# Issuing the last SiLU and product of an up chunk behind the copy of the next chunk's first product

## The chip, the core and the metric

The program runs on one core of a Trainium2 chip. The metric is the device time of one execution in microseconds, lower being better. A core has TensorE (PE, the matrix multiplier, with PEld for its weight loads), VectorE (DVE), ScalarE (ACT), GpSimd (POOL) and SyncE (SP), each with its own queue worked off in order; an instruction that waits holds up everything behind it on its engine. Results of TensorE land in PSUM, which VectorE and ScalarE read; everything else is in SBUF.

## The reference

The program is an encoder trunk of two layers over 768 tokens (512 of one request, 256 of another), with 1024 features. Each layer is `x += 1/2 FFN(norm(x)); x += mixer(norm(x)); x += 1/2 FFN(norm(x))`; the mixers are a gated linear recurrence and a windowed attention. The four feed-forwards are what matters here:

```python
def swiglu_ffn(x, w1, w2):
    gate, up = jnp.split(x @ w1, 2, axis=-1)      # w1: 1024 x 5632
    return (jax.nn.silu(gate) * up) @ w2          # w2: 2816 x 1024
```

Everything is float32. The kernel splits each operand into a high and a low part and multiplies three times (high by high, high by low, low by high).

## The kernel before

**Tiling.** The 2816 hidden features are 22 chunks of 128. A feed-forward (`ffn`, L510) goes through five groups of four chunks and then two more chunks. A group computes the hidden values of its four chunks ("up"), and then multiplies them into the output ("down", `down_quad`, L465). The first two chunks of a feed-forward are computed plainly; every later one by `up_pair` (L431), which makes seven products of half the depth (p1, p7, p2, p5, p4, p6, p3, in this order) in place of eight. So a full group has four calls of `up_pair`, here called its chunks 1 to 4; the first group has only chunks 3 and 4.

**One chunk.** A product is twelve matmuls of 128x384 (L422). Products accumulate in four PSUM banks a, b, c, d, and some banks are read in the middle: ScalarE copies bank a after p1 (L439, "the copy") because p2 goes on accumulating in the same bank, so p2's first matmul waits for the copy; likewise c after p7 (L442). After p6, VectorE combines the banks (L452 to L454), giving the first half's hidden value t. After p3 come L457 and L459 on VectorE, the SiLU of the second half on ScalarE (L460) and its product on VectorE (L461), giving w.

**After a chunk.** Each half is split into high and low (ScalarE L267, then VectorE L268). After two chunks `gather` calls `mix`, four VectorE subtractions (L351, L352, L354, L355) over the four halves with three more splits, giving the combined operands t1 to t4 that "down" takes.

**Down.** Seven products of 18 matmuls of 128x512 (L486), in the order p1, p2, p5, p4, p7, p6, p3 of the source. VectorE adds each partial result into x (L508). p2 goes on accumulating in p1's banks, and p4 in p5's, so p2's first matmul waits for the first L508 on p1, and p4's for that on p5.

**Weights.** Each weight block is loaded by SP into one of four raw buffers `wr` (L155), then staged into one of eight tiles `w`: ScalarE makes the high part (L203), VectorE the low part (L204; for p5 of an up chunk it is GpSimd). Some products need sums of blocks: two VectorE additions in the raw buffer (L217: one for p6, then one for p3), and additions made by DMAs that POOL issues (L145). A raw buffer is loaded anew when the last reader of its block is done: for an up chunk that is the L204 of p3. The four raw buffers of a "down" are filled while chunks 2 to 4 run. The third weight of "down" (p5's) is a sum that POOL's DMA makes from the third and the fourth raw buffer.

**What sets the order.** The instructions are written in program order and a scheduler places them on each engine's queue by when it takes them to be ready; `issue_after` adds an order between two instructions without a wait. `up_pair` is a generator: it yields t and later w, and the caller splits and gathers between.

Of the kernel before, what the change touches and what calls it, by code (L numbers as in the profile page):

```python
# [12 lines left out]
AF = mybir.ActivationFunctionType  # L13
# [35 lines left out]
class Trunk:  # L49
    def __init__(self, ctx, tc, consts):  # L50
        self.tc, self.nc = tc, tc.nc
        pool = lambda name, **kw: ctx.enter_context(tc.tile_pool(name=name, bufs=1, **kw))
        self.cp = pool("consts")
        self.xp = pool("xp")
        self.wp = pool("wp")
        self.tp = pool("tp")
        self.sp = pool("stats")
        self.ap = pool("arena")
        self.pp = pool("psum", space=bass.MemoryType.PSUM)
        self.dp = pool("dram", space=bass.MemoryType.DRAM)  # L60
        self.uid = 0
        self.deferred = []
        self.queue, self.loaded, self.staged, self.held = [], [], {}, 0
        self.setup(consts)

# [362 lines left out]
                    skip_group_check=True,  # L428
                )

    def up_pair(self, tag, j):  # L431
        nc = self.nc
        key = (tag, j)
        a, b, c, d = (self.ps(H) for _ in range(4))
        v, w, t = (self.tmp(H) for _ in range(3))
        p = lambda name, ps, first, last: self.product(key, name, FACTOR[name], ps, first, last)
        free = lambda *names: [self.done((*key, name)) for name in names]
        p("p1", a, True, False)
        nc.scalar.copy(v, a)  # L439
        free("p1")  # L440
        p("p7", c, True, False)
        nc.scalar.copy(w, c)  # L442
        free("p7")
        p("p2", a, False, True)
        nc.scalar.activation(a, a, AF.Silu)
        free("p2")
        p("p5", d, True, False)
        nc.vector.tensor_sub(w, w, d)
        free("p5")
        p("p4", c, False, True)  # L450
        p("p6", b, True, True)
        nc.vector.tensor_sub(v, v, b)  # L452
        nc.vector.tensor_sub(t, c, v)
        nc.vector.tensor_mul(t, t, a)  # L454
        free("p4", "p6")
        yield t
        nc.vector.tensor_sub(w, w, v)  # L457
        p("p3", d, False, True)
        nc.vector.tensor_add(v, v, d)  # L459
        self.last_act = nc.scalar.activation(v, v, AF.Silu).ins  # L460
        self.last_dve = nc.vector.tensor_mul(w, v, w).ins  # L461
        free("p3")
        yield w

    def down_quad(self, tag, g, hid):  # L465
        nc = self.nc
# [43 lines left out]
    def ffn(self, tag, next_row):  # L510
        for g in range(GROUPS):
            hid = {}

            def put(name, src, kp):
                if name not in hid:
                    hid[name] = self.big([P, 2, 2, H], F32R)
                self.split(src, hid[name][:, kp, 0, :], hid[name][:, kp, 1, :])

            def gather(ts, kp):
                self.mix(ts[0], ts[1], ts[2], ts[3], lambda name, src: put(name, src, kp))  # L520

            if g == 0:
                ts = {}
                for half in range(2):
                    for j in range(PLAIN):
                        t = ts[2 * j + half] = self.up_plain(tag, j, half)
                        name = f"b{j}{half}"
                        if name != "b01":
                            put(name, t, 0)
                gather(ts, 0)  # L530
                self.run_later(len(self.deferred))
            for kp in range(2):
                if g == 0 and kp == 0:
                    continue
                ts = []
                for j in range(2):
                    for half, t in enumerate(self.up_pair(tag, 4 * g + 2 * kp + j)):
                        ts.append(t)
                        name = f"b{j}{half}"
                        if name != "b01":  # L540
                            put(name, t, kp)
                gather(ts, kp)
            self.down_quad(tag, g, hid)
        hids = []
        for j in range(NF - 2, NF):
            hid = self.big([P, 2, T], F32R)
            for half, t in enumerate(self.up_pair(tag, j)):
                self.split(t, *(hid[:, i, half * H : (half + 1) * H] for i in range(2)))
            hids.append(hid)
        if next_row is None:  # L550
            self.load_final()
        banks = {}

        def add(b, k, hid):
            sl = slice(b * P, (b + 1) * P)
            for c in range(2):
                wh, wl = self.take((tag, "last", c))
                if k == 0:
                    banks[(b, c)] = self.ps()
                w = wh[:, k, :], wl[:, k, :]  # L560
                self.mm3(banks[(b, c)], (hid[:, 0, sl], hid[:, 1, sl]), w, k == 0, k == 1)
                if b == NBLK - 1 and k:
                    self.done((tag, "last", c))

        for b in range(NBLK):
            for i, k in (((0, 0), (1, 0), (0, 1)), ((1, 1),))[b] if b < 2 else ((b, 0), (b, 1)):
                add(i, k, hids[k])
            for c in range(2):
                self.add_x(self.x[b][:, c * 512 : (c + 1) * 512], banks[(b, c)], 0.5)
            self.after_block(b, next_row)  # L570
            if b >= 4:
                self.run_later()
# [773 lines left out]
```

## Time and profile before

| | |
|---|---|
| median of 3 runs | 2764.35 us (2763.74 to 2765.22) |
| the profiled execution's own time | 2764.33 us |
| its span, first to last instruction | 2762.5 us |
| granted TensorE clock | 0.999 |
| PE busy | 2735.5 us, 99% of the span |
| PEld busy | 2481.5 us, 90% |
| DVE busy | 2102.6 us, 76% |
| ACT busy | 1326.6 us, 48% |
| POOL busy | 309.4 us, 11% |

The span is 1.8 us shorter than the execution's time; that rest lies outside the first and last instruction. A row of a timeline gives the start from the span's beginning in us, how long the row lasts, engine, line, operation, what is written from what, a count where equal rows that follow each other are merged, and in brackets how long the engine sat idle before it and what released it. The names: `ps` are PSUM banks, `tA` the half-chunk values (v, w, t in the code), `big` the split operands, `w`, `wr`, `s` the staged, raw and summed weights.

### The profile page before, as it was taken

What the parts mean: (1) busy time and instruction counts of PE and PEld (TensorE: products, weight loads), DVE (VectorE), ACT (ScalarE), POOL (GpSimd) and SP (SyncE); (2) the same over time, 40 slices, a digit from 0 to 9 for tenths busy, and PEclk for the clock granted to TensorE, in tenths of its full rate; (3) what the DMA queues carried; (4) which work ended last, traced back from release to release, by engine and by line L of the source; (5) the groups of instructions that cost most, each with busy time, mean ns of one, the idle gap of its engine ahead of it and who ended that gap; (6) DMA issues with size and microseconds to landing.
All of it is one profiled execution on the core that took longest, in us unless ns stands there. A gap on an engine that the chain in (4) does not pass through costs nothing.

```text
span 2762.5 us, 44483 instructions
## 1 busy us (share of the span) xinstructions
PE 2735.5 (99%) x17281; PEld 2481.5 (90%) x17281; DVE 2102.6 (76%) x3662; ACT 1326.6 (48%) x2479; POOL 309.4 (11%) x315
## 2 busy tenths in 40 slices
PE   8999999999999999999999999999999999999998
PEld 8999999888888889999999999999886789999997
DVE  7888788557477568777888878887846768788877
ACT  7444444456466354443446444444546654443444
POOL 1111211000000001121111112111000001221111
PEclk9999999999999999999999999999999999999999
DMA  5544554321110324465444355544512123555443
GB/s 160 135 117 116 138 134 119 118 67 40 55 47 25 122 62 114 112 143 133 118 120 109 83 131 138 133 115 115 146 53 77 47 62 81 134 137 128 120 112 107
DMA packets 330116, 291.63 MB, mean 106 GB/s; under 512 B 11608, under 2 KB 257840, under 8 KB 329904
## 3 DMA queue, kind: packets, MB, share of 16 engines
q1 hardware_dynamic: 294064, 212.43, 25.8%
q0 software_dynamic: 31680, 62.93, 13.4%
q10 hardware_dynamic: 4160, 13.42, 1.4%
q8 instruction: 135, 2.21, 0.3%
q14 instruction: 77, 0.63, 0.1%
HBM read 216.39 MB, written 9.44 MB: 82 GB/s over the span
## 4 chain that ended last, share of the span: by engine, by line
PE 85%; DVE 10%; ACT 3%; issue 2%; DMA 0%; DVEq 0%; ACTq 0%; SPq 0%
PE ps L422 32%; PE ps L486 21%; PE ps L262 9%; PE ps L263 9%; PE ps L264 9%; DVE w L204 2%; DVE big L268 2%; PE ps L682 1%; PE ps L1218 1%; PE ps L1157 1%; PE ps L827 1%; PE ps L1209 1%; ACT w L203 1%; DVE wr L217 1%; PE ps L324 1%
## 5 line engine op out<-in xcount | busy, mean ns | idle before, releaser
L422 PE MATMUL ps<-big,w 128*128 128x384 f32 x6720 | 1174.6, 335 | 3.4 <-ACT tA L439 2.7
L422 PEld LDWEIGHTS ps<-big,w 128*128 128x128 f32 x6720 | 1165.4, 188 | 10.9 <-ACT tA L439 9.1
L203 ACT CAST w<-wr 128x512 fp32r<-128x512 f32 x600 | 415.3, 707 | 699.8 <-DVE wr L217 376.3
L204 DVE TENSOR_TENSOR w<-wr,w 128x512 fp32r<-128x512 f32 (+1 forms) x520 | 452.8, 874 | 180.1 <-ACT w L203 153.9
L486 PE MATMUL ps<-w,big 128*128 128x512 f32 x2520 | 575.9, 389 | 1.2 <-DVE x L508 1.2
L486 PEld LDWEIGHTS ps<-w,big 128*128 128x128 f32 x2520 | 472.4, 188 | 99.6 <-ACT big L267 1.6
L508 DVE SCALAR_TENSOR_TENSOR x<-ps,x 128x512 f32<-128x512 f32 x468 | 303.5, 680 | 10.5 <-PE ps L264 10.0
L145 POOL DMA_DIRECT2D s<-wr x120 | 105.0, 875 | 1667.5 <-DMA wr<-in_ffn_w_dram 784.5
L262 PE MATMUL ps<-w,big 128*128 128x512 f32 x624 | 252.5, 405 | 0.3
L264 PE MATMUL ps<-w,big 128*128 128x512 f32 x624 | 244.6, 392 | 0.9 <-DVE big L331 0.9
L263 PE MATMUL ps<-w,big 128*128 128x512 f32 x624 | 244.4, 392 | 0.0
L262 PE MATMUL ps<-big,w 128*128 128x384 f32 (+2 forms) x640 | 219.2, 344 | 2.1 <-ACT big L267 1.3
L267 ACT CAST big<-tA 128x384 fp32r<-128x384 f32 x296 | 148.0, 513 | 149.3 <-DVE tA L454 69.0
L263 PE MATMUL ps<-big,w 128*128 128x384 f32 (+2 forms) x640 | 216.4, 338 | 0.9 <-DVE big L268 0.6
L264 PE MATMUL ps<-big,w 128*128 128x384 f32 (+2 forms) x640 | 215.6, 337 | 0.0
L268 DVE TENSOR_TENSOR big<-tA,big 128x384 fp32r<-128x384 f32 x296 | 183.0, 629 | 12.7 <-ACT big L267 11.6
L171 DVE TENSOR_TENSOR w<-wr,w 128x1024 fp32r<-128x1024 f32 x92 | 111.8, 1221 | 79.0 <-ACT w L170 73.1
L262 PEld LDWEIGHTS ps<-w,big 128*128 128x128 f32 x624 | 117.2, 188 | 29.3 <-issue 6.0
L170 ACT CAST w<-wr 128x1024 fp32r<-128x1024 f32 x92 | 96.5, 1052 | 97.8 <-PE ps L263 77.8
L204 POOL TENSOR_TENSOR w<-wr,w 128x512 fp32r<-128x512 f32 x80 | 123.3, 1541 | 177.5 <-ACT w L203 156.4
L264 PEld LDWEIGHTS ps<-w,big 128*128 128x128 f32 x624 | 117.1, 188 | 27.6 <-DVE big L331 1.7
L263 PEld LDWEIGHTS ps<-w,big 128*128 128x128 f32 x624 | 117.4, 188 | 21.8 <-issue 0.4
(163 smaller groups left out, 2899.6 us busy)
## 6 DMA issues: line engine op xcount, KB each, us to landing
wr<-in_ffn_w_dram SPq DMA_DIRECT2D x264, 512.0 KB, 3.9
s<-in_ffn_w_dram SPq DMA_DIRECT2D x120, 256.0 KB, 3.3
s<-wr POOLq DMA_DIRECT2D x120, 256.0 KB, 4.5
wr<-wr POOLq DMA_DIRECT2D x80, 256.0 KB, 3.7
wr<-in_hg_w_in_dram SPq DMA_DIRECT2D x40, 512.0 KB, 3.8
wr<-wr POOLq DMA_DIRECT2D x20, 512.0 KB, 4.6
spill<-x ACTq DMA_DIRECT2D x12, 512.0 KB, 2.7
x<-spill ACTq DMA_DIRECT2D x12, 512.0 KB, 3.3
```

What stands on the lines that cost most here:

```text
L145: self.nc.gpsimd.dma_start(out, src, accum_op=ALU.add)
L171: self.nc.vector.tensor_sub(lo, raw, hi.bitcast(F32))
L203: nc.scalar.copy(h, src)
L204: low = (eng or nc.vector).tensor_sub(l, src, h.bitcast(F32)).ins
L262: nc.tensor.matmul(out, a[0], b[0], start=first, stop=False)
L263: nc.tensor.matmul(out, a[0], b[1], start=False, stop=False)
L264: nc.tensor.matmul(out, a[1], b[0], start=False, stop=last)
L267: self.nc.scalar.copy(hi, src)
L268: self.nc.vector.tensor_sub(lo, src, hi.bitcast(F32))
L422: self.nc.tensor.matmul(ps, a[x], b[y], start=first and k == 0 and i == 0, stop=k == 3 and i == 2, skip_group_check=True,)
L486: nc.tensor.matmul(ps, a[x], w[y], start=name == chain and kp == 0 and q == 0, stop=kp == 1 and q == 2, skip_group_check=True,)
L508: self.nc.vector.scalar_tensor_tensor(x, ps, c, x, ALU.mult, ALU.add)
```

## The change

`up_pair` no longer is a generator. The SiLU of its second half goes into a list `tail`, and so do the product, its split and, after an even chunk, the whole gather. The next chunk's `up_pair` issues the list right behind its own copy of p1; each part on ScalarE must come after that copy in the queue. Behind the last chunk ahead of a "down", and behind the last chunk of a feed-forward, the list is issued at once. No computation is added or removed.

```diff
+    def run_tail(self, after=None):
+        for call in self.tail:
+            with self.tc.issue_after(after) if after else nullcontext():
+                call()
+        self.tail = []
+
-    def up_pair(self, tag, j):
+    def up_pair(self, tag, j, then):
...
         p("p1", a, True, False)
-        nc.scalar.copy(v, a)
+        turned = nc.scalar.copy(v, a).ins
         free("p1")
+        self.run_tail(turned)
         p("p7", c, True, False)
...
         free("p4", "p6")
-        yield t
+        then(0, t)
         nc.vector.tensor_sub(w, w, v)
         p("p3", d, False, True)
         nc.vector.tensor_add(v, v, d)
-        self.last_act = nc.scalar.activation(v, v, AF.Silu).ins
-        self.last_dve = nc.vector.tensor_mul(w, v, w).ins
+
+        def silu():
+            self.last_act = nc.scalar.activation(v, v, AF.Silu).ins
+
+        def rest():
+            self.last_dve = nc.vector.tensor_mul(w, v, w).ins
+            then(1, w)
+
+        self.tail = [silu]
         free("p3")
-        yield w
+        return rest
...
-                    for half, t in enumerate(self.up_pair(tag, 4 * g + 2 * kp + j)):
+                    def then(half, t, j=j, kp=kp, ts=ts):
                         ts.append(t)
                         name = f"b{j}{half}"
                         if name != "b01":
                             put(name, t, kp)
-                gather(ts, kp)
+                        if len(ts) == 4:
+                            gather(ts, kp)
+
+                    rest = self.up_pair(tag, 4 * g + 2 * kp + j, then)
+                    self.tail.append(rest)
+            self.run_tail()
             self.down_quad(tag, g, hid)
...
-            for half, t in enumerate(self.up_pair(tag, j)):
+            def then(half, t, hid=hid):
                 self.split(t, *(hid[:, i, half * H : (half + 1) * H] for i in range(2)))
+            rest = self.up_pair(tag, j, then)
+            self.tail.append(rest)
             hids.append(hid)
+        self.run_tail()
```

The order of the instructions on TensorE, POOL and SP stays as it was; on ScalarE and VectorE it changes at the chunk boundaries of the feed-forwards. The rows below are from the second group of the first feed-forward; the others read alike. The changed kernel's line numbers are shifted: its L446 is the copy (L439 before), L470 the SiLU (L460), L473 the product (L461), L467 the addition after p3 (L459), L456 is L448, L460 to L465 are L452 to L457, L352 to L356 the four subtractions of the gather (L351 to L355), L204 and L205 the high and low part of a weight (L203, L204), L218 the weight sums (L217), L268 and L269 the two halves of a split (L267, L268).

ScalarE, from chunk 3 into chunk 4, before (`w_223` is the weight of chunk 4's p3, `w_237` that of the coming down's p1, `big_189` chunk 3's t, `ps_230` chunk 4's bank a):

```order
L203 CAST w_223_1478<-wr_186_1198 128x512
L203 CAST w_237_1534<-wr_224_1481 128x1024
L267 CAST big_189_1206<-tA_217_1381 128x384
L460 ACTIVATE tA_215_1379<-tA_215_1379 128x384
L439 COPY tA_234_1518<-ps_230_1514 128x384
L442 COPY tA_235_1519<-ps_232_1516 128x384
```

The same place now:

```order
L204 CAST w_223_1478<-wr_186_1198 128x512
L204 CAST w_237_1532<-wr_224_1481 128x1024
L268 CAST big_189_1206<-tA_212_1360 128x384
L446 COPY tA_234_1516<-ps_230_1512 128x384
L470 ACTIVATE tA_210_1358<-tA_210_1358 128x384
L450 COPY tA_235_1517<-ps_232_1514 128x384
```

The copy has changed places with the SiLU of chunk 3; both still stand behind two weight casts and the split of chunk 3's t.

VectorE at the start of chunk 3, before (`w_218` and `w_219` are weights of chunk 4's p7 and p2; `big_206` is the split of chunk 2's product, `big_207` that of t1):

```order
L459 TENSOR_TENSOR tA_195_1232<-tA_195_1232,ps_194_1231 128x384
L204 TENSOR_TENSOR w_205_1353<-wr_186_1198,w_205_1353 128x512
L268 TENSOR_TENSOR big_204_1334<-tA_197_1234,big_204_1334 128x384
L461 TENSOR_TENSOR tA_196_1233<-tA_195_1232,tA_196_1233 128x384
L204 TENSOR_TENSOR w_218_1395<-s3_188_1202,w_218_1395 128x512
L268 TENSOR_TENSOR big_206_1356<-tA_196_1233,big_206_1356 128x384
L351 TENSOR_TENSOR tA_196_1233<-tA_178_1097,tA_196_1233 128x384
L352 TENSOR_TENSOR tA_178_1097<-tA_179_1098,tA_178_1097 128x384
L204 TENSOR_TENSOR w_219_1411<-wr_186_1198,w_219_1411 128x512
L354 TENSOR_TENSOR tA_179_1098<-tA_179_1098,tA_196_1233 128x384
L268 TENSOR_TENSOR big_207_1361<-tA_178_1097,big_207_1361 128x384
L355 TENSOR_TENSOR tA_197_1234<-tA_197_1234,tA_179_1098 128x384
```

Now:

```order
L467 TENSOR_TENSOR tA_195_1230<-tA_195_1230,ps_194_1229 128x384
L205 TENSOR_TENSOR w_205_1351<-wr_186_1198,w_205_1351 128x512
L269 TENSOR_TENSOR big_204_1334<-tA_197_1232,big_204_1334 128x384
L205 TENSOR_TENSOR w_213_1374<-s3_188_1202,w_213_1374 128x512
L473 TENSOR_TENSOR tA_196_1231<-tA_195_1230,tA_196_1231 128x384
L269 TENSOR_TENSOR big_214_1379<-tA_196_1231,big_214_1379 128x384
L205 TENSOR_TENSOR w_219_1411<-wr_186_1198,w_219_1411 128x512
L352 TENSOR_TENSOR tA_196_1231<-tA_178_1097,tA_196_1231 128x384
L353 TENSOR_TENSOR tA_178_1097<-tA_179_1098,tA_178_1097 128x384
L355 TENSOR_TENSOR tA_179_1098<-tA_179_1098,tA_196_1231 128x384
L269 TENSOR_TENSOR big_215_1384<-tA_178_1097,big_215_1384 128x384
L356 TENSOR_TENSOR tA_197_1232<-tA_197_1232,tA_179_1098 128x384
```

The product has gone behind one weight, and the first two subtractions behind another.

VectorE later in chunk 3, before (`w_221` to `w_223` are the weights of chunk 4's p4, p6 and p3; L217 makes the sums for the last two):

```order
L448 TENSOR_TENSOR tA_216_1380<-tA_216_1380,ps_214_1378 128x384
L204 TENSOR_TENSOR w_221_1443<-wr_187_1200,w_221_1443 128x512
L217 TENSOR_TENSOR wr_186_1198<-wr_186_1198,wr_187_1200 128x512
L204 TENSOR_TENSOR w_222_1474<-wr_186_1198,w_222_1474 128x512
L217 TENSOR_TENSOR wr_186_1198<-wr_186_1198 128x512
L452 TENSOR_TENSOR tA_215_1379<-tA_215_1379,ps_212_1376 128x384
L453 TENSOR_TENSOR tA_217_1381<-ps_213_1377,tA_215_1379 128x384
L204 TENSOR_TENSOR w_223_1478<-wr_186_1198,w_223_1478 128x512
L454 TENSOR_TENSOR tA_217_1381<-tA_217_1381,ps_211_1375 128x384
L457 TENSOR_TENSOR tA_216_1380<-tA_216_1380,tA_215_1379 128x384
L459 TENSOR_TENSOR tA_215_1379<-tA_215_1379,ps_214_1378 128x384
```

Now:

```order
L269 TENSOR_TENSOR big_216_1389<-tA_197_1232,big_216_1389 128x384
L269 TENSOR_TENSOR big_217_1392<-tA_196_1231,big_217_1392 128x384
L269 TENSOR_TENSOR big_218_1395<-tA_179_1098,big_218_1395 128x384
L218 TENSOR_TENSOR wr_186_1198<-wr_186_1198,wr_187_1200 128x512
L460 TENSOR_TENSOR tA_210_1358<-tA_210_1358,ps_207_1355 128x384
L205 TENSOR_TENSOR w_222_1474<-wr_186_1198,w_222_1474 128x512
L461 TENSOR_TENSOR tA_212_1360<-ps_208_1356,tA_210_1358 128x384
L218 TENSOR_TENSOR wr_186_1198<-wr_186_1198 128x512
L462 TENSOR_TENSOR tA_212_1360<-tA_212_1360,ps_206_1354 128x384
L465 TENSOR_TENSOR tA_211_1359<-tA_211_1359,tA_210_1358 128x384
L205 TENSOR_TENSOR w_223_1478<-wr_186_1198,w_223_1478 128x512
L467 TENSOR_TENSOR tA_210_1358<-tA_210_1358,ps_209_1357 128x384
```

The gather's last three splits, which stood ahead of L448, now stand behind L456 and `w_221`; the second weight sum stands behind two of the chunk's own operations, and the weight of p3 behind four where it was behind two.

More of the change, by code (lines that the diff above doesn't have):

```diff
@@ L429, in product @@
                 )
-    def up_pair(self, tag, j):
+    def run_tail(self, after=None):
+        for call in self.tail:
+            with self.tc.issue_after(after) if after else nullcontext():
+                call()
+        self.tail = []
+    def up_pair(self, tag, j, then):
         nc = self.nc
```

## The prediction

> **What bounds the kernel now.** First the page: TensorE is busy nearly all the time, so a gain can only come from the little time in which it stands still, while a loss can come from any engine that begins to keep it waiting.
>
> ```profile
> span 2762.5 us, 44483 instructions
> PE 2735.5 (99%) x17281; PEld 2481.5 (90%) x17281; DVE 2102.6 (76%) x3662; ACT 1326.6 (48%) x2479; POOL 309.4 (11%) x315
> ```
>
> Then the waits of the two TensorE rows, for the operation that is moved:
>
> ```profile
> PE ps L422 <- ACT tA L439: 2.7, 11, 0.4
> ...
> PEld ps L422 <- ACT tA L439: 9.1, 19, 0.8
> ```
> ```profile
> L422 PE MATMUL ps<-big,w 128*128 128x384 f32 x6720 | 1174.6, 335 | 3.4 <-ACT tA L439 2.7
> ```
>
> The copy after p1 does hold up TensorE: 2.7 us by the matmul row, 9.1 us in 19 places by the weight-load row. Matmuls overlap in the records (335 ns each, but 1174.6 / 6720 = 175 ns apart), so a stall has to outlast the overlap before PE shows idle; I take 9.1 us as the most that the change can bring. [...]
>
> Third, the timeline of one such place, chunk 4 of the first feed-forward's second group:
>
> ```profile
> 157.01 0.68 DVE L217 TENSOR_TENSOR wr<-wr 128x512 f32<-128x512 f32 x1
> ...
> 157.81 1.58 ACT L203 CAST w<-wr 128x512 fp32r<-128x512 f32 x2 [1.44 <-DVE wr L217]
> ...
> 158.67 0.68 DVE L204 TENSOR_TENSOR w<-wr,w 128x512 fp32r<-128x512 f32 x1
> 159.27 0.55 DVE L454 TENSOR_TENSOR tA<-tA,ps 128x384 f32<-128x384 f32 x1
> 159.38 0.37 SPq L155 DMA_DIRECT2D wr<-in_ffn_w_dram  x1
> ...
> 159.85 0.51 ACT L267 CAST big<-tA 128x384 fp32r<-128x384 f32 x1 [0.47 <-DVE tA L454]
> 160.39 0.56 DVE L459 TENSOR_TENSOR tA<-tA,ps 128x384 f32<-128x384 f32 x1
> ...
> 160.98 0.53 ACT L460 ACTIVATE tA<-tA 128x384 f32<-128x384 f32 x1 [0.61 <-DVE tA L459]
> ...
> 161.41 0.46 ACT L439 COPY tA<-ps 128x384 f32<-128x384 f32 x1
> ...
> 161.92 0.64 PEld L422 LDWEIGHTS ps<-big,w 128*128 128x128 f32 x4 [0.50 <-ACT tA L439]
> 161.92 0.79 PE L422 MATMUL ps<-big,w 128*128 128x384 f32 x3 [0.18 <-ACT tA L439]
> ```
>
> The copy waits for chunk 3's SiLU, and that for a VectorE that is late. So VectorE's lateness in chunk 3 is the true cause, and the change both takes the copy out from behind it and rearranges that very stretch of VectorE.
>
> **What the change wins.** It issues nothing more and nothing less; TensorE, POOL and SP keep their order. Alone, putting the copy ahead of the SiLU would let it start when the split of t has been issued, near 160.3 instead of 161.41: over 1 us earlier against a stall of 0.50, so the stall would be gone. But the copy still stands behind the two weight casts and the split, and these come later, because VectorE gets there later. I walk chunk 3 forward from its own copy at 145.13, with the durations of these rows.
>
> ```profile
> 144.26 0.53 ACT L460 ACTIVATE tA<-tA 128x384 f32<-128x384 f32 x1
> ...
> 145.13 0.48 ACT L439 COPY tA<-ps 128x384 f32<-128x384 f32 x1 [0.35 <-PE ps L422]
> 145.22 0.55 DVE L461 TENSOR_TENSOR tA<-tA,tA 128x384 f32<-128x384 f32 x1
> 145.51 0.62 ACT L203 CAST w<-s 128x512 fp32r<-128x512 f32 x1
> ...
> 147.21 0.48 ACT L442 COPY tA<-ps 128x384 f32<-128x384 f32 x1 [0.67 <-PE ps L422]
> 147.36 0.56 DVE L351 TENSOR_TENSOR tA<-tA,tA 128x384 f32<-128x384 f32 x1
> ...
> 149.50 0.55 DVE L268 TENSOR_TENSOR big<-tA,big 128x384 fp32r<-128x384 f32 x1
> 149.68 0.61 ACT L203 CAST w<-wr 128x512 fp32r<-128x512 f32 x1
> ...
> 149.97 0.55 DVE L355 TENSOR_TENSOR tA<-tA,tA 128x384 f32<-128x384 f32 x1
> ...
> 150.99 1.62 POOL L204 TENSOR_TENSOR w<-wr,w 128x512 fp32r<-128x512 f32 x1
> 151.10 2.87 DVE L268 TENSOR_TENSOR big<-tA,big 128x384 fp32r<-128x384 f32 x3 [0.58 <-ACT big L267]
> ...
> 154.96 0.68 DVE L217 TENSOR_TENSOR wr<-wr,wr 128x512 f32<-128x512 f32 x1
> ...
> 156.40 0.69 DVE L204 TENSOR_TENSOR w<-wr,w 128x512 fp32r<-128x512 f32 x1 [0.76 <-ACT w L203]
> ```
>
> Before, the SiLU ran ahead of the copy at 144.26, with nobody waiting. Now it runs behind the copy and a weight cast, 146.03 to 146.56; the product goes from 145.22 to 146.77. Its split then waits on ScalarE for the copy of c, which TensorE frees at 147.21: cast to 148.10, VectorE's part to 148.68. The weight behind it ends at 149.35, the first subtraction starts at 149.27 (147.36 before), the third ends at 150.88. The cast for t1 stands behind the one that ends at 150.29, and ends at 150.96.
>
> So t1's split on VectorE, which ran at 149.50, now arrives at 150.99, just as GpSimd's weight subtraction starts. Before, the next split fell into it: three splits took 2.87 us instead of about 0.55 + 2 x 0.47 = 1.49 (0.47 is the step from 149.50 to 149.97), so one was held for about 1.4 us, and the next two started near 153. I take it that t1's split is held in its place until 153.03. The fourth subtraction, L448, `w_221` and three splits follow to 155.97, the first weight sum runs at 155.90 (154.96 before), L452 from 156.50, the weight behind it ends at 158.03, L453 at 158.50, and the second weight sum at 159.10, against 157.01 + 0.68 = 157.69: 1.4 us later. The gain of filling a wait of 0.76 us before that weight is in this.
>
> ScalarE then casts p3's weight from 159.21 to 159.83, the 1024-wide one to 160.79, t to 161.21, and copies from 161.12 to 161.58. Before, the copy ended at 161.87. So it is 0.3 us earlier, not 1 us. The longest stall stands elsewhere, in the first feed-forward's first group:
>
> ```profile
> 74.59 0.47 PEld L422 LDWEIGHTS ps<-big,w 128*128 128x128 f32 x3 [0.75 <-ACT tA L439]
> ```
>
> The program has four feed-forwards with four groups each in which chunk 4 follows a deferred gather: 16 x 0.3 = 4.8 us. That stall of 0.75 us has no deferred gather ahead of it and goes wholly: 5.6 in all. TensorE's restart behind a stall is part of the 9.1 and partly goes too, so the gain lies between 5.6 and 9.1; I take **6.5 us**.
> **What it costs.** Behind L457 the low part of p3's weight now ends near 160.64 instead of 158.67 + 0.68 = 159.35, that is **1.28 us later**. It is the last reader of a raw buffer, and SP's load stands at 159.38, 0.03 us behind its end: the fourth block of the coming down. What hangs on it, in the same group:
>
> ```profile
> 168.32 1.05 ACT L203 CAST w<-wr 128x1024 fp32r<-128x1024 f32 x1 [3.51 <-DMA wr<-wr]
> 169.40 1.23 DVE L204 TENSOR_TENSOR w<-wr,w 128x1024 fp32r<-128x1024 f32 x1 [2.44 <-ACT w L203]
> 170.57 0.56 DVE L452 TENSOR_TENSOR tA<-tA,ps 128x384 f32<-128x384 f32 x1
> ...
> 175.20 0.68 DVE L508 SCALAR_TENSOR_TENSOR x<-ps,x 128x512 f32<-128x512 f32 x1
> ```
>
> The load feeds the adding DMA, for which ScalarE's cast waits 3.51 us, for which VectorE's L204 waits 2.44 us; and behind that L204 stand chunk 4's L452 to L461, a weight and the first L508 of down, which p2's first matmul needs. None of these has moved in the queue, so all of them come 1.28 us later. On SP and POOL nothing is moved past anything, so no further cost is added there.
>
> What TensorE pays for a late L204 can be read in this trace: in the group whose down starts at 1249.97 the adding DMA itself was slow. Its rows, and the two downs side by side from their first matmul to the next group's:
>
> ```profile
> 1247.88 2.00 ACT L203 CAST w<-wr 128x1024 fp32r<-128x1024 f32 x2 [5.56 <-DMA wr<-wr]
> 1248.97 1.23 DVE L204 TENSOR_TENSOR w<-wr,w 128x1024 fp32r<-128x1024 f32 x1 [4.48 <-ACT w L203]
> 1249.97 4.28 PE L486 MATMUL ps<-w,big 128*128 128x512 f32 x18
> ...
> 1255.46 24.94 PE L486 MATMUL ps<-w,big 128*128 128x512 f32 x108 [1.20 <-DVE x L508]
> ```
> ```profile
> 172.46:201.06 28.60, 28.60 (x128) 23.65 (x128) 27.53 (x44) 9.56 (x16) 4.73 (x5) 1.00 0.51 129
> 1249.97:1280.24 30.27, 29.07 (x127) 23.50 (x127) 28.89 (x47) 9.51 (x16) 4.46 (x5) 1.00 0.53 122
> ```
>
> There L204 started 1.00 us before the down, in the usual group 172.46 - 169.40 = 3.06 before: 2.06 us later, and the down took 30.27 - 28.60 = **1.67 us longer**. So TensorE pays all but 0.39 us of what L204 is late against it. VectorE is busy 27.53 of 28.60 us in a down (its column is the third), so it has nothing to catch up with.
>
> In the changed kernel L204 is 1.28 us later and TensorE comes about 0.35 earlier (the 0.3 and a part of the restart): 1.63 us late, cost 1.63 - 0.39 = 1.24 us a group. The four first groups have no deferred gather ahead of chunk 4 and pay nothing; 16 groups pay 16 x 1.24 = 19.8 us. Bounds: nothing, if the slack covers all, and 16 x 1.67 = 26.7 us, if every group is as late as the one seen.
>
> **Sum.** 19.8 - 6.5 = +13.3 us. The profiled execution took 2764.33 us (span 2762.5 and 1.8 around it), 0.02 below the median: 2764.35 + 13.3 = 2777.6, I say **2777.5 us**.
>
> **Rivals.**
> (a) The loss doesn't come: SP's load or the DMA has room that the rows hide, and only the gain is left, 2764.35 - 6.5 = 2757.9 (down to 2755.3 with all of 9.1). For it speaks that the stall is real; against it that SP's load starts 0.03 us behind L204's end, and that each link shows a wait for the one before.
> (b) GpSimd's hold falls on one operation later. If t1's split gets in first (it misses by hundredths of a us), the fourth subtraction is held instead, and all behind it gains 0.47 us: late by 0.81, cost 0.81 + 0.35 - 0.39 = 0.77 a group, 16 x 0.77 - 6.5 = +5.8, 2770.2. [...]
> (c) Late chains add up: the DMA, issued into other traffic, takes as long as in the slow group, 5.56 against 3.51 us of waiting; late by 2 us, 16 x (2 + 0.35 - 0.39) - 6.5 = +24.9, 2789.
> (d) Gain and loss cancel: late by 0.45 us, since 16 x (0.45 + 0.35 - 0.39) = 6.6. That needs two thirds of my shift to be wrong.
> That the change doesn't do what it says is excluded by the order: the copy does stand ahead of the SiLU.
>
> **How the numbers follow.** The forecast 0.60; (a) 0.14, (b) 0.12, (c) 0.06, (d) 0.08. A measurement of this kernel tells 0.2%, 5.5 us, from no change. Slower by more: forecast, (b) and (c), 0.78. Faster by more: (a) but for 0.01 of it, 0.13. Within: the rest, 0.09. The range leaves out (a) and (c), 0.20 together: from 2763, just below no change, to 2784, which allows 1.64 us a group.
>
> **What would show it.** The wait of L422 for the copy falls from 9.1 us to about 2. A wait of L486 for DVE x L508 appears in some 16 groups, about 0.8 to 1.2 us each at p2, and a smaller one at p4. VectorE's wait at the 1024-wide L204 for ScalarE's cast grows from 2.44 us to more than 3, and SP's load comes over 1 us later behind the copy of chunk 3. Wrong would be: no new L508 waits (rival a), or the second L217 less than 0.5 us later (d).

## The result

The changed kernel takes 2784.39 us (median of 5 runs, 2782.58 to 2787.47) against 2764.59 us for the kernel before in the same runs: a ratio of 1.0074, 95% interval 1.0062 to 1.0086. It is slower by about 20 us; 2777.5 was forecast, and 2784.39 lies just outside the range.

The page of the changed kernel, span and busy times, then three rows of its waits, and last VectorE's wait of before that belongs to the first of them:

```profile
span 2782.6 us, 44483 instructions
...
PE 2742.4 (99%) x17281; PEld 2483.1 (89%) x17281; DVE 2096.4 (75%) x3662; ACT 1321.6 (47%) x2479; POOL 309.6 (11%) x315
```
```profile
DVE w L205 <- ACT w L204: 193.8, 220, 5.3
...
PE ps L501 <- DVE x L523: 16.2, 16, 2.0
...
PEld ps L423 <- ACT tA L446: 2.6, 10, 0.6
```
```profile
DVE w L204 <- ACT w L203: 160.3, 217, 4.5
```

The wait for the copy fell from 9.1 us to 2.6, and VectorE waits 193.8 us for ScalarE's weight casts where it waited 160.3. "Down" has a new wait, which before came once: TensorE for VectorE's first add, 16 times, 16.2 us by the matmul row. All 16 stand at p2; the smaller wait at p4 that was forecast beside them did not come. The timeline of the second group of the first feed-forward, which the prediction walked through, shows how:

```profile
150.17 1.62 POOL L205 TENSOR_TENSOR w<-wr,w 128x512 fp32r<-128x512 f32 x1
150.25 1.97 DVE L269 TENSOR_TENSOR big<-tA,big 128x384 fp32r<-128x384 f32 x1
...
157.60 0.68 DVE L218 TENSOR_TENSOR wr<-wr 128x512 f32<-128x512 f32 x1
...
159.14 0.69 DVE L205 TENSOR_TENSOR w<-wr,w 128x512 fp32r<-128x512 f32 x1
...
160.28 0.48 ACT L446 COPY tA<-ps 128x384 f32<-128x384 f32 x1
...
160.66 0.53 ACT L470 ACTIVATE tA<-tA 128x384 f32<-128x384 f32 x1
...
164.14 0.88 POOL L146 DMA_DIRECT2D wr<-wr  x1 [12.34 <-ACT ps L453]
...
169.95 2.00 ACT L204 CAST w<-wr 128x1024 fp32r<-128x1024 f32 x2 [6.27 <-DMA wr<-wr]
...
171.03 1.23 DVE L205 TENSOR_TENSOR w<-wr,w 128x1024 fp32r<-128x1024 f32 x1 [5.19 <-ACT w L204]
...
177.52 4.81 PE L501 MATMUL ps<-w,big 128*128 128x512 f32 x13 [1.92 <-DVE x L523]
```

t1's split arrives 0.08 us behind the start of GpSimd's subtraction and is held: 1.97 us for an operation of 0.56. The low part of p3's weight ends at 159.83, and the rest of the chain follows to p2's matmul at 177.52.

The windows view by stretch gives the account: its length, the busy time of PE, PEld, DVE, ACT and POOL with their counts, the granted clock, the DMA share and GB/s. Quoted are an up stretch, its down, 3.41 us inside that down, a usual down, and 3.41 us in the attention:

```profile
112.97:171.32 58.35, 58.35 (x337) 58.21 (x336) 42.03 (x68) 26.77 (x50) 10.25 (x11) 1.00 0.52 127
171.32:203.73 32.41, 30.49 (x127) 24.78 (x127) 31.47 (x50) 10.96 (x18) 4.73 (x5) 0.95 0.50 121
178.34:181.75 3.41, 3.41 (x10) 2.68 (x9) 3.41 (x8) 1.56 (x4) 0.00 (x0) 0.50 0.22 67
438.70:468.24 29.54, 29.05 (x128) 23.53 (x127) 29.49 (x48) 10.34 (x17) 4.79 (x5) 1.00 0.55 131
...
2096.64:2100.05 3.41, 3.41 (x18) 3.05 (x19) 2.17 (x10) 1.09 (x3) 0.00 (x0) 0.50 0.52 154
```

Cut at the first matmul of each "down" and of what follows it, the profiled executions differ from that of before (span 2762.5) as in this table, in us; each run is described below, and the last column is its median time.

| run | ahead of first down | 16 up stretches | 20 downs | rest, mostly attention | span | time |
|---|---|---|---|---|---|---|
| the change | -1.0 | -5.2 | +24.7 | +1.6 | +20.1 | 2784.39 |
| e1, gather not deferred | -1.3 | -8.1 | +3.0 | +1.4 | -5.0 | 2759.31 |
| e2, only the gather's tail deferred | -0.1 | -4.8 | +22.9 | +1.9 | +19.9 | 2783.44 |
| e3, the change, other load order | +0.4 | -5.5 | -1.1 | +1.7 | -4.4 | 2758.45 |
| e4, before, other load order | -0.3 | +1.1 | -1.8 | +0.1 | -0.9 | 2763.38 |
| e5, e1 and e3 together | -0.9 | -8.1 | -1.8 | +0.1 | -10.7 | 2753.62 |
| e6, the change, no GpSimd subtraction | -1.3 | -8.1 | 0.0 | +1.1 | -8.2 | 2756.07 |
| e9, before, no GpSimd subtraction | -0.7 | -8.1 | -1.8 | +0.8 | -9.8 | 2754.19 |
| e10, e5 and e6 together | -1.0 | -8.1 | -1.8 | +0.1 | -10.7 | 2753.59 |
| e7, before, adding DMA 2.46 us late | +0.2 | +0.6 | +43.0 | 0.0 | +43.8 | 2808.11 |
| e8, before, adding DMA 3.9 us late | +0.5 | -0.8 | +85.2 | +0.1 | +85.0 | 2849.28 |

### The profile page after: what moved, and what is told of

It is laid out like the page before. It is cut to its first block, busy times and chain, and to the rows that moved or that the text cites. A ratio compares the mean times of both kernels' runs of the same rounds, so it can differ in the third digit from the quotient of the medians.

```text
span 2782.6 us, 44483 instructions
## 1 busy us (share of the span) xinstructions
PE 2742.4 (99%) x17281; PEld 2483.1 (89%) x17281; DVE 2096.4 (75%) x3662; ACT 1321.6 (47%) x2479; POOL 309.6 (11%) x315
## 3 DMA queue, kind: packets, MB, share of 16 engines
q0 software_dynamic: 31680, 62.93, 13.3%
## 4 chain that ended last, share of the span: by engine, by line
PE 88%; DVE 6%; DMA 3%; ACT 2%; issue 1%; ACTq 0%; DVEq 0%; SPq 0%
PE ps L423 37%; PE ps L501 19%; PE ps L263 9%; PE ps L265 9%; PE ps L264 9%; DMA wr<-wr 2%; DVE w L205 1%; PE ps L708 1%; PE ps L1244 1%; PE ps L1183 1%; PE ps L1235 1%; PE ps L853 1%; ACT w L204 1%; DVE x L523 1%; PE ps L325 1%
## 5 line engine op out<-in xcount | busy, mean ns | idle before, releaser
L204 ACT CAST w<-wr 128x512 fp32r<-128x512 f32 x600 | 414.6, 707 | 699.0 <-DVE wr L218 348.1
L501 PE MATMUL ps<-w,big 128*128 128x512 f32 x2520 | 585.6, 393 | 16.2 <-DVE x L523 16.2
L205 DVE TENSOR_TENSOR w<-wr,w 128x512 fp32r<-128x512 f32 (+1 forms) x520 | 447.5, 864 | 193.1 <-ACT w L204 179.3
L501 PEld LDWEIGHTS ps<-w,big 128*128 128x128 f32 x2520 | 473.0, 189 | 123.7 <-ACT big L268 22.7
L268 ACT CAST big<-tA 128x384 fp32r<-128x384 f32 x296 | 147.9, 513 | 185.3 <-DVE tA L462 76.6
L269 DVE TENSOR_TENSOR big<-tA,big 128x384 fp32r<-128x384 f32 x296 | 180.7, 621 | 21.0 <-ACT big L268 18.0
L263 PEld LDWEIGHTS ps<-w,big 128*128 128x128 f32 x624 | 117.5, 188 | 29.3 <-issue 5.9
L205 POOL TENSOR_TENSOR w<-wr,w 128x512 fp32r<-128x512 f32 x80 | 123.4, 1543 | 174.0 <-ACT w L204 153.2
L265 PEld LDWEIGHTS ps<-w,big 128*128 128x128 f32 x624 | 117.4, 188 | 27.5 <-DVE big L332 1.7
L146 POOL DMA_DIRECT2D wr<-wr x100 | 87.3, 873 | 465.0 <-ACT ps L453 181.9
```

Of the source, the lines that this page charges most:

```text
L146: self.nc.gpsimd.dma_start(out, src, accum_op=ALU.add)
L204: nc.scalar.copy(h, src)
L205: low = (eng or nc.vector).tensor_sub(l, src, h.bitcast(F32)).ins
L263: nc.tensor.matmul(out, a[0], b[0], start=first, stop=False)
L265: nc.tensor.matmul(out, a[1], b[0], start=False, stop=last)
L268: self.nc.scalar.copy(hi, src)
```

## The experiments

Theory: the gather, moved into chunk 3, makes the low part of p3's weight late; with it come the load of a block, the adding DMA and VectorE, and p2 of "down" waits. The rivals sit elsewhere: the SiLU and product that moved into chunk 4, or a VectorE that is overloaded whatever the load does.

**e1: without the deferred gather.** Line 562 of the changed kernel, where the tail of an even chunk now is issued at once:

```diff
-                    self.tail.append(rest)
+                    self.tail.append(rest) or (self.run_tail() if j else None)
```

> The change without the deferred gather: the tail of chunks 1 and 3 (SiLU, product, its split) goes behind the next chunk's copy, the tail of chunk 2, which holds the gather, is issued at once as before. My theory (the loss comes from the gather moved into chunk 3, the gain from the copy put ahead of the SiLU): no down gets longer (28.60 us each, the one slow group apart), the up stretches keep the gain, since the copy of chunk 4 now stands ahead of the SiLU while VectorE in chunk 3 is as early as before; 2758 us, 2755.5 to 2760. Rival (the SiLU, product and split that land in chunk 4 make VectorE late for the down by themselves): p2's first matmul still waits in some 16 downs, 2775 us or more. Third possibility (the gain too depends on the gather): no gain, 2763 to 2766.

Measured: 2759.31 us, 0.9979 (0.9970 to 0.9988). The start of chunk 4 in the timeline, then an up stretch and its down in the windows view:

```profile
159.31 0.47 ACT L446 COPY tA<-ps 128x384 f32<-128x384 f32 x1
159.43 0.55 DVE L467 TENSOR_TENSOR tA<-tA,ps 128x384 f32<-128x384 f32 x1
...
160.02 0.53 ACT L470 ACTIVATE tA<-tA 128x384 f32<-128x384 f32 x1 [0.23 <-DVE tA L467]
```
```profile
112.78:171.05 58.27, 58.27 (x338) 58.27 (x336) 44.25 (x71) 27.65 (x50) 10.24 (x11) 1.00 0.51 127
171.05:199.85 28.80, 28.80 (x128) 23.51 (x127) 28.75 (x47) 10.34 (x17) 4.79 (x5) 1.00 0.59 136
```

The copy starts before VectorE has even made what the SiLU waits for, and no stall is left: 58.27 us in all 16 up stretches. So the SiLU and product in chunk 4 are not the loss. But the downs are not free, as had been expected: 3.0 us in all, 0.20 in this one. TensorE reaches them 0.48 us earlier and VectorE does not, so the slack of 0.39 us is used up.

**e2: only the gather's tail.** The other half, in the same line:

```diff
-                    self.tail.append(rest)
+                    self.tail.append(rest) or (None if j else self.run_tail())
```

> The other half: only the tail of chunk 2 (SiLU, product, split, gather) goes behind the copy of chunk 3; chunks 1 and 3 keep the order of before. My theory: the low part of p3's weight in chunk 3 ends some 1.2 us later as in the changed kernel, but TensorE gains nothing at chunk 4's copy, so the down is late by about 1.2 us and pays 1.2 - 0.39 = 0.8 us in 16 groups, some more where the adding DMA is slow: 2764.4 + 13 to 20 = 2780 us, 2775 to 2787. Rival (the loss needs the tail of chunk 3 in chunk 4): downs of 28.60 us, 2763 to 2766 us.

Measured: 2783.44 us, 1.0065 (1.0053 to 1.0078); the downs lose 22.9 us. That is the loss of the change with chunk 3's tail issued at once, so the tail of chunk 2, with the gather in it, does it. My reason for the up stretches failed: they gain 4.8 us here too, since the scheduler put the copy ahead of the SiLU in this kernel by itself, as its timeline shows:

```profile
161.09 0.47 ACT L446 COPY tA<-ps 128x384 f32<-128x384 f32 x1
...
161.46 0.52 ACT L470 ACTIVATE tA<-tA 128x384 f32<-128x384 f32 x1
```

So e2 is nearly the whole change, and e1 is what separates the halves.

**e3: another load order in the changed kernel.** The blocks of a "down" are loaded in the order first, third, fourth, second, so that the load which waits for p3's weight no longer feeds the adding DMA. All engines keep their order; what changes is which block a load brings.

```diff
-        for src in srcs:
+        for src in [srcs[i] for i in ((0, 2, 3, 1) if len(srcs) == 4 else range(len(srcs)))]:
...
-            steps = self.quad_steps(key, raws, srcs, how)
+            steps = self.quad_steps(key, raws if len(raws) == 2 else [raws[i] for i in (0, 3, 1, 2)], srcs, how)
```

> The changed kernel, with the four blocks of a down loaded in the order first, third, fourth, second: the load that waits for p3's weight is then that of the second block, which p2's weight is cast from directly, and no longer an input of the adding DMA. Order of TensorE, VectorE, ScalarE, POOL and SP otherwise as in the changed kernel. My theory (late weight, late load, late adding DMA, late VectorE, p2 waits): the 1024-wide weight subtraction is no longer late, no down waits for its first add, the gain of the up stretches stays: 2759 us, 2756.5 to 2761.5. Rival (VectorE has more than it can do behind the hold by GpSimd, whatever the load does): downs still 1.0 us longer, 2776 us or more. Rival 2 (p2's weight becomes what is late): p2's first matmul waits for ScalarE or VectorE's weight instead, 2770 to 2785.

Measured: 2758.45 us, 0.9975 (0.9966 to 0.9984). The same group in the timeline, and its down:

```profile
161.36 0.88 POOL L146 DMA_DIRECT2D wr<-wr  x1 [8.38 <-DMA wr<-in_ffn_w_dram]
...
167.47 1.05 ACT L204 CAST w<-wr 128x1024 fp32r<-128x1024 f32 x1 [1.17 <-DMA wr<-wr]
...
168.61 1.23 DVE L205 TENSOR_TENSOR w<-wr,w 128x1024 fp32r<-128x1024 f32 x1 [0.97 <-PE ps L423]
```
```profile
172.52:201.12 28.60, 28.60 (x127) 23.65 (x127) 28.54 (x46) 10.36 (x17) 4.79 (x5) 1.00 0.58 139
```

The adding DMA is issued 11.16 us ahead of the down instead of 171.32 - 164.14 = 7.18, the 1024-wide subtraction starts 3.91 us ahead instead of 0.29, and the downs are 28.60 us again but for two (0.4 each). The adding DMA itself is no faster: it now runs beside a load and takes 5.9 us from issue to landing here, against 4.6 in a usual group of the change. VectorE's order and work are those of the change, so the loss runs through the load, as the theory had it; the rival of an overloaded VectorE falls.

**e4: the same load order in the kernel before.** The edit is that of e3.

> The kernel before with the same order of loads. My theory: no down of the kernel before waits but the one with the slow adding DMA (1.67 us), so this brings 0 to 1.7 us: 2762.7 to 2764.6. By the rival that the order of loads is worth something for itself (another 5 us or more from elsewhere), 2759 or less, and the result of the same order in the changed kernel would have to be read against it.

Measured: 2763.38 us, 0.9994 (0.9985 to 1.0002), no change that can be told. In the profiled execution the slow group is gone (30.27 to 28.60 us). The order of loads is worth almost nothing here, where nothing is late.

**e5: e1 and e3 together.**

> Both repairs together: the gather is not deferred, and the down's blocks are loaded in the order first, third, fourth, second. My theory: the up stretches are as short as with the gather not deferred (58.27 us each instead of 58.75, and 1.2 us in front of the first down), and the downs are all 28.60 us, so the 2.9 us that these lost there (they were reached earlier with VectorE no earlier) are back, as is the 1.7 us of the slow group: 2764.4 - 1.2 - 16 x 0.48 - 1.8 = 2753.7 us, 1.6 more if TensorE's clock is halved in the attention again; 2752.5 to 2756.5. Rival (the two gains are one and the same time): 2758 to 2759.5.

Measured: 2753.62 us, 0.9960 (0.9947 to 0.9972). An up stretch and its down:

```profile
112.82:171.09 58.27, 58.27 (x338) 58.27 (x336) 44.28 (x72) 27.80 (x50) 10.04 (x10) 1.00 0.52 127
171.09:199.69 28.60, 28.60 (x128) 23.65 (x127) 28.55 (x46) 10.29 (x17) 4.79 (x5) 1.00 0.57 139
```

All 16 and all 20 read like this. The two gains add up, so the copy's wait and the late adding DMA are two things.

**e6: no GpSimd subtraction.** The changed kernel with the low part of p5's weight on VectorE, 80 operations more there:

```diff
-            low = split(name, own[name], nc.gpsimd if up and name == "p5" else None)
-            if not (up and name == "p5"):
+            low = split(name, own[name], None)
+            if True:
                 last[0] = low
```

> The changed kernel with the low part of p5's weight of an up chunk on VectorE instead of GpSimd, so that no GpSimd operation reads SBUF beside the gather's splits. VectorE has one 128x512 operation more per chunk (about 0.6 us). My theory (the 1.6 us by which the down is late contain the hold of about 1.4 us by GpSimd's weight): the lateness falls by 1.4 - 0.6 = 0.8 us, the downs of 16 groups lose 0.4 us each instead of 1.3 and TensorE's clock isn't halved in them: 2784.4 - 14 = 2770 us, 2763 to 2776. Rival (the gather's own work is what is late, the hold falls into a wait anyway): the downs lose 0.6 us more each, 2794 us or more.

Measured: 2756.07 us, 0.9968 (0.9954 to 0.9981), far below the range. The timeline of chunk 3 (t1's split, the low part of p3's weight) and the down behind it:

```profile
149.68 0.56 DVE L269 TENSOR_TENSOR big<-tA,big 128x384 fp32r<-128x384 f32 x1
...
157.24 0.69 DVE L205 TENSOR_TENSOR w<-wr,w 128x512 fp32r<-128x512 f32 x1
```
```profile
170.67:199.28 28.61, 28.61 (x127) 23.62 (x127) 26.73 (x44) 9.62 (x16) 3.48 (x4) 1.00 0.55 136
```

The split takes 0.56 us, and p3's weight ends 12.74 us ahead of the down instead of 171.32 - 159.83 = 11.49: 1.25 us earlier, where I had expected 0.8. That is nearly the whole hold, 1.97 - 0.56 = 1.41 us, so the added operation cost little. The scheduler also put the first weight sum ahead of the last three splits in this kernel, so e6 alone does not separate the hold from the order; e9 does.

**e7 and e8: the adding DMA made late in the kernel before.** ScalarE copies the fourth block onto itself ahead of the adding DMA, twice at full width (e7), and once more at half width (e8):

```diff
-        self.into(a21, a22)
+        any(nc.scalar.copy(a22, a22) is None for _ in range(0 if up else 2)) or self.into(a21, a22)
```

> The kernel before with two ScalarE copies of the down's fourth block onto itself (128x1024, 1.05 us each) ahead of the adding DMA: nothing else moves, the adding DMA is 2.2 us later in all 20 groups. My theory: each down is 2.2 - 0.39 = 1.8 us longer, 20 x 1.8 = 36 us, 2800 us (2795 to 2806); the stall at p2 is below the 2.08 us at which the clock was halved, so no down has matmuls of 427 ns, but where the adding DMA is slow too. Rival (slack is larger than read from the one slow group): 20 x 1.2 or less, below 2790. Rival 2 (the clock is halved by lower stalls too): 2812 or more, with matmuls of 427 ns in 7 or more downs.

> As the run with two copies, with a third one of half size behind the cast of p2's weight: the adding DMA is about 3.4 us later, the stall at p2 about 3.0 us. My theory: the clock is halved when one window of a fixed grid of 3.41 us has TensorE idle for more than about 2.1 us of it; a stall of 3.0 us leaves such a window in (3.0 - 0.95) / 3.41 = 60% of all positions, so 8 to 16 of 20 downs run about eight matmuls at 427 ns and lose 1.7 us more: 2764.4 + 20 x 3.0 + 12 x 1.7 = 2845 us (2832 to 2856). Rival (the halving belongs to a slow adding DMA or to these two groups, not to the stall): at most 3 downs with 427 ns, 2824 or less. Rival 2 (any stall over 2.1 us halves it, wherever the grid stands): all 20 downs, 2858.

Measured, one run each: 2808.11 us, above the 2795 to 2806 expected, and 2849.28, inside its range. In e7 the DMA is issued 6.46 us ahead of a usual down (8.92 before), so 2.46 us later, not 2.2; such a down takes 2.07 us more, which is 2.46 - 0.39. Two downs also had their clock halved, where none was expected.

The price read from the one slow group holds. Add to what a down takes beyond 28.60 us the lead that ScalarE's cast of the DMA's sum has over the down: for the slow group that is 1.67 + (1249.97 - 1247.88) = 3.76. In all downs that wait at full clock, of before, of the change and of e7, this sum lies between 3.74 and 3.79, so each us by which that cast is late costs TensorE one us. In the four downs with a halved clock, two of the change and two of e7, it is 5.18 (171.32 of the change: 3.81 + 171.32 - 169.95). A halved stretch thus costs such a down 1.4 us, somewhat less than half its length.

Two downs of e7 with their first rows behind the stall, windows and timeline:

```profile
265.62:298.36 32.74, 30.48 (x128) 24.72 (x128) 32.26 (x50) 11.29 (x19) 4.77 (x5) 0.95 0.50 122
...
1681.19:1712.83 31.64, 29.06 (x127) 23.50 (x127) 30.95 (x50) 11.41 (x19) 4.78 (x5) 1.00 0.52 120
```
```profile
272.15 8.23 PE L486 MATMUL ps<-w,big 128*128 128x512 f32 x28 [2.26 <-DVE x L508]
```
```profile
1688.05 4.12 PE L486 MATMUL ps<-w,big 128*128 128x512 f32 x17 [2.58 <-DVE x L508]
```

The first stalls for 2.26 us and has its clock halved (0.95 over the down), the second stalls for longer, 2.58 us, and keeps its full clock. Between the start and the end of the program each halved stretch of the change lasts 3.41 us at a granted clock of 0.50, and so does that of this first down, from 273.22 to 276.63. In the change they start at 178.34, 2096.64 and 2437.97, which is 562 and 100 times 3.413 us apart; in e7 at 181.06 and 273.22, 27 times. The borders that lie whole multiples of 3.413 us from such a start are the grid meant here, and a window is the time between two of them. The second stall lies across a border of it (0.9 us in one window, 1.7 in the next), the first inside one window. In e8, 17 of 20 downs were halved, more than the 8 to 16 expected: with 92.16 us from one to the next, 27 windows, the groups fall into step with the grid, so that positions are not spread evenly. The down at 1189.09 stalled for 2.73 us across a border (1.9 us in one window, 0.9 in the next) and was spared; the one at 85.57 was not:

```profile
1189.09:1220.71 31.62, 28.89 (x127) 23.57 (x127) 30.35 (x47) 11.27 (x18) 4.71 (x5) 1.00 0.46 117
85.57:119.00 33.43, 30.45 (x128) 24.71 (x128) 31.66 (x49) 12.02 (x19) 4.76 (x5) 0.95 0.49 118
```
```profile
1196.33 8.91 PE L486 MATMUL ps<-w,big 128*128 128x512 f32 x38 [2.73 <-DVE x L508]
```

So not every long stall has a halved stretch behind it, and not every one of these groups. In the two halved downs of the change, stalls of 1.92 and 2.01 us lie inside one window; the stalls of its other downs that lie inside one are 1.35 us (the matmul at 1669.60) or less, and that of 1.56 us (at 1261.36) lies across a border. The edge is not sharp by the matmul rows. Two windows of down, one of e7 that a halved one followed and one of e8 that none did, are filled alike, 1.57 and 1.56 us:

```profile
177.64:181.06 3.42, 1.57 (x7) 1.05 (x6) 3.42 (x6) 1.88 (x5) 0.00 (x0) 1.00 0.21 55
```
```profile
1192.03:1195.45 3.42, 1.56 (x7) 0.95 (x6) 3.42 (x7) 0.99 (x2) 0.00 (x0) 1.00 0.00 0
```

**e9: no GpSimd subtraction in the kernel before.** The edit is that of e6.

> The kernel before with the low part of p5's weight on VectorE instead of GpSimd, and the tails not deferred: what this edit is worth for itself, against which its worth in the changed kernel is to be read. My theory (GpSimd's hold of 1.4 us per chunk made VectorE late also before, and with it the SiLU and the copy of chunk 4): the copy waits less or not at all and the downs stay at 28.60 us, 2764.9 - 16 x 0.3 - 1 = 2759 us, 2756 to 2762; the changed kernel is then worth another 2 to 4 us on top of it (2756.1). Rival (the hold cost nothing before): 2764 to 2767. Rival 2 (the extra operation on VectorE costs where it is fully used, in the downs' neighbourhood): 2768 or more.

Measured: 2754.19 us, 0.9958 (0.9945 to 0.9970), below the range of 2756 to 2762 and no slower than e6, which was expected to gain 2 to 4 us on top of it. The added operation and the three splits of chunk 3, chunk 4's start, and the up stretch:

```profile
149.78 0.69 DVE L204 TENSOR_TENSOR w<-wr,w 128x512 fp32r<-128x512 f32 x1
150.44 1.50 DVE L268 TENSOR_TENSOR big<-tA,big 128x384 fp32r<-128x384 f32 x3
...
158.36 0.56 DVE L459 TENSOR_TENSOR tA<-tA,ps 128x384 f32<-128x384 f32 x1
...
158.95 0.53 ACT L460 ACTIVATE tA<-tA 128x384 f32<-128x384 f32 x1 [0.49 <-DVE tA L459]
...
159.38 0.46 ACT L439 COPY tA<-ps 128x384 f32<-128x384 f32 x1
```
```profile
113.05:171.32 58.27, 58.27 (x337) 58.26 (x336) 45.11 (x78) 27.70 (x50) 6.05 (x7) 1.00 0.49 123
```

VectorE's order in this chunk is that of before but for the added operation, which stands where VectorE waited 0.58 us ahead of the three splits. These take 1.50 us where they took 2.87, and what follows, counted from the start of the up stretch, is 1.4 us earlier (L457 at 157.71 - 113.05 = 44.66 us against 159.73 - 113.71 = 46.02). The copy still stands behind the SiLU, and TensorE does not stall. So the hold was also why VectorE, the SiLU and the copy were late before; the wait that the change attacks is a consequence of it, and without the hold the change has nothing left to win.

**e10: all three.**

> Tails deferred but for the gather's, the down's blocks loaded in the order first, third, fourth, second, and p5's low part on VectorE. My theory: in the run with the first two of these the up stretches are at 58.27 us and the downs at 28.60 us, with no wait left that the third could take, so no change against its 2753.6 us: 2752.5 to 2755.5. Rival (VectorE's free time is worth something elsewhere): below 2751. Rival 2 (its extra operation costs): 2758 or more.

Measured: 2753.59 us, 0.9958 (0.9944 to 0.9971), as e5 and e9. All three have the same 58.27 and 28.60 us. The smallest edit among them is that of e9, two lines in the kernel before.

## Why the prediction was right and wrong

The direction was right, and the time was 6.9 us too low. Step by step:

- **The gain, 6.5 us: right.** The wait at the copy fell by 9.1 - 2.6 = 6.5 us, and the up stretches with the part ahead of the first down gained 6.2.
- **The walk through chunk 3: right.** Counted from the first matmul of its up stretch, the low part of p3's weight ended at 45.64 us before (159.35 - 113.71) and at 46.86 now (159.83 - 112.97): 1.22 us later (forecast 1.28). TensorE came 58.75 - 58.35 = 0.40 us earlier (forecast 0.35, with a part of a restart in it that no row shows by itself). The hold fell on t1's split in 13 of 16 groups; on the operation before it in one, on a later one in two. Rival (b), the hold on a later operation, came in those two; their downs lost 0.93 and 1.11 us, the forecast for it being 0.77.
- **The price, 1.24 us a group: right where nothing came on top.** Eleven of the 16 groups lost 0.93 to 1.35 us, 1.18 on average.
- **"16 groups at 1.24 us" is the step that failed.** The term came to 24.7 us instead of 19.8. The sum took every group to be alike, put no cost on POOL ("no further cost is added there") and had no step for TensorE's clock. Two downs lost 3.8 and 3.9 us: their adding DMA was slow, as in the one slow group of before, now on top of the lateness. They stalled for 1.92 and 2.01 us by the matmul rows, and TensorE's clock was halved for a window of 3.41 us in each, which cost 1.4 us there (see e7). Two more lost 1.7 and 1.8: one again with a slow DMA, the other with a DMA of usual speed issued 6.78 us ahead of its down, where a usual group has 7.1 to 7.5. The group that was slow before lost 0.3 more, and the first down of all 0.2. Rival (c) had the slow DMA in all groups; it came in four.
- **What no step had: the attention.** Its 1.6 us is a third halved window (the row at 2096.64). Its work was not touched; in the window ahead of the halved one matmuls fill 1.92 of 3.42 us. It happened in the profiled run of e1, e2, e3 and e6, and in none of e4, e5, e9 and e10. That the position on the grid decides this is argued from e7 and e8, not shown. How much of the window is filled does not decide alone (last section). What decides stays open.
- **Sum.** -6.2 + 24.7 + 1.6 = 20.1. The three halved windows are about 4.4 of it (1.4, 1.4 and 1.6); without them the change would have cost 15.7, against the forecast of 13.3.
- **Rivals (a) and (d)**, no loss or a cancelled one, are out: the L501 waits came, and the second weight sum was late.

What I read too lightly was the hold itself. The prediction used its 1.4 us only to place the splits; e6 and e9 show that without it neither the old stall nor the new loss is left.

## What to carry to other kernels

Ask why the engine that a copy waits for is late before reordering around it: here two lines that moved GpSimd's subtraction to VectorE, so that the two no longer met, took 2754.19 us in the kernel before and needed none of the reordering, which took 2784.39. When a step is deferred, follow what it delays to the last reader of each buffer, because the load that waits there can feed another engine a stage later; here the order of loads decided whether it mattered, 2784.39 us against 2758.45 in e3. And price stalls group by group rather than by a mean: two of 1.92 and 2.01 us had a halved clock behind them, 1.4 us on top in each.

## What the runs showed of the hardware

**The halved clock.** The stretches of 3.41 us with a granted clock of 0.50, and the multiples of 3.413 us between their starts, are told at e7. Ahead of a halved one stood a stall of 1.92 us inside one window in the down at 171.32 of the change, and one of 2.26 in that at 265.62 of e7; a stall of 2.58 us across a border, in the down at 1681.19 of e7, had none behind it. The windows ahead of halved ones were partly used, with matmuls in 1.57 of 3.42 us in a down of e7 and 1.92 of 3.42 in the attention of the change.

How far a window is filled with matmuls does not decide alone. These are the windows ahead of the halved one in the attention of the change and of e3, and one of e10 that is filled less and was followed by none:

```profile
2093.22:2096.64 3.42, 1.92 (x14) 0.88 (x16) 3.38 (x12) 2.58 (x6) 0.00 (x0) 1.00 0.56 210
```
```profile
2076.91:2080.32 3.41, 2.04 (x16) 0.99 (x18) 3.41 (x11) 2.47 (x6) 0.00 (x0) 1.00 0.54 188
```
```profile
2071.17:2074.58 3.41, 1.85 (x14) 0.78 (x12) 2.38 (x8) 3.41 (x11) 0.00 (x0) 1.00 0.76 260
```

**The adding DMA and instruction packets.** The adding DMA is the same 144 packets each time. The DMA view of two stretches of the changed kernel, from issue to just short of the cast, a usual group (254.95 to 259.75) and the one whose down starts at 2431.61 (2424.17 to 2430.32); the columns of the last row of each are count, size and time from issue to landing:

```profile
q0 software_dynamic: 144, 0.52, 57.4%
...
wr<-wr POOLq DMA_DIRECT2D x1, 512.0 KB, 4.6
```
```profile
q0 software_dynamic: 144, 0.52, 45.5%
q8 instruction: 1, 0.02, 1.0%
...
wr<-wr POOLq DMA_DIRECT2D x1, 512.0 KB, 6.0
```

One packet of 16 KB of an instruction queue ran beside it. In the profiles of before and of the change, the 31 adding DMAs of feed-forwards that no packet of an instruction queue overlapped took 2.76 to 2.78 us from their first packet to their last, and the 9 that one overlapped, of 16 KB in eight and of 8 KB in one, 2.85 to 4.29. No run moved those packets, so it is not shown that they are the cause. Two cases fall outside: one of e2 took 3.08 us with none beside it (the group whose down starts at 1255.29), one of e9 2.77 with one (171.32).
